# Score products of 64-dim heads over all 128 rows of the tensor engine, in two attention blocks of a four-layer kernel

## The chip, the core and the metric

The kernel runs on one core of a Trainium2 chip. The metric is the time of one execution in microseconds (us); less is better. The engines are named as the profile names them: PE (tensor engine, matmuls; PEld is its weight loads), DVE (vector engine), ACT (scalar engine), POOL (GpSimd), SP (the engine that issues DMAs). SBUF is the on-chip memory, PSUM the memory into which PE accumulates; both have 128 partitions.

## What is computed

The input is one sequence of 512 tokens with 1024 features. A first block (softmax attention, a gated delta rule, a gate) is left alone by the change. After it come two layers, each an attention and a feed-forward part (gate, up and down projection, 2816 wide), all in float32. The two attentions are what the change touches:

```python
# layer 0: stick breaking, 16 heads of 64; per block of 128 queries
z = einsum('bqhd,bkhd->bhqk', q_blk, k) * 64 ** -0.5
earlier = key_pos[None, :] < q_pos[:, None]
log_keep = where(earlier, log_sigmoid(-z), 0.0)
log_after = cumsum(log_keep, axis=3, reverse=True) - log_keep
weight = where(earlier, exp(log_sigmoid(z) + log_after), 0.0)
out = einsum('bhqk,bkhd->bqhd', weight, v)

# layer 1: differential attention, 8 heads with two maps of 64 dims each, values of 128
a = softmax(q1 k1 / 8) - lam * softmax(q2 k2 / 8)     # visible: key chunk of 64 <= query chunk
out = einsum('bhqk,bkhd->bqhd', a, v)                  # then an rms norm over the head
```

## The kernel before

**Matmuls in parts.** A product of float32 operands is made of three products in the type float32r: each operand is split into a rounded part `hi` and a rest `lo`, and `hi hi + hi lo + lo hi` accumulate in one PSUM bank (`mm3`, L307). `split` (L314) makes `hi` by a copy on ACT and `lo` by a subtraction on DVE. Weights come from DRAM as 512 KB tiles by DMAs on SP's queue and are split in the same way (`wtile`, L322). A few products, such as the one with the values, are plain float32, for which PE has two rows in the trace, each with a weight load.

**Order of the work.** Each part of a layer is a set of generators ("streams"). A `Driver` (L87) runs them in one thread at build time and so fixes the order of PE's instructions: it keeps a model clock, adds a cost for each matmul (L293), and always continues the stream that is ready first by that clock, the streams listed first before the others. A stream yields a number (us until its next operands are there), an event, or a place of a resource (PSUM banks: 2 for projections, 5 called `z`, 1 called `o`). So `SB_LAT1 = 5.0` and `DF_LAT1 = 4.0` are what the order allows for the elementwise work between two of a unit's PE steps. The projections are the last stream of each block: they fill PE's time between the attention steps. Nothing at run time changes this order; an engine works its instructions off in order, each waiting for its semaphores. Tiles of 128 x 512 float32 ("chunks") come from one pool of 57.

**Stick breaking** (`stick`, L601). Two heads (a pair `hp`, 8 pairs) share one chunk of 128 features: the head `s` = 0 has partitions 0 to 63, the head 1 has 64 to 127. A projection of q or k is evacuated in `evac_qk`: a multiply by the norm on DVE (L614), `hi` on ACT (L615), `lo` on DVE (L616), so each pair has four chunks (`sb_qhi`, `sb_qlo`, `sb_khi`, `sb_klo`). The event of the pair is set 2.6 us after its key projection (L660). The values are projected for four heads at once with tokens on partitions (`evac_v`, L620; for the first `first_v`, L626); ACT scales them (`scale_tm`, L571).

A `unit` (L664) handles one head and a bank of key tiles: b = 2 holds the key tiles 2 and 3 (256 and 128 query columns), b = 1 tile 1 (384), b = 0 tile 0 (512). For each key tile it makes the scores, three products of 64 rows and a mask (L680 to L683):

```python
self.mm(zz, k[0][d, ks], q[0][d, P * i:], j == 0, False)     # d: the head's 64 partitions
self.mm(zz, k[0][d, ks], q[1][d, P * i:], False, False)
self.mm(zz, k[1][d, ks], q[0][d, P * i:], False, False)
self.mm(zz[:, :P], self.neg30, self.m_ge, False, False)
```

Then come three functions on ACT (L686 to L688), a combination on DVE (L689) and a split into `sh` and `sl` on DVE; after `SB_LAT1` the sums over later keys are made on PE by triangular and all-minus-one matrices (L701, L703) in the same bank, ACT takes the exponential (L705), and PE multiplies by the values (L717) into the pair's `po` bank, each head into its own 64 partitions, with 64 columns of weights.

**Differential attention** (`diff`, L1814). q and k are projected with tokens on partitions, normed and rotated (`rotate`), transposed on PE in `to_fm` (L1892) and split there on ACT (L1902) and DVE (L1903); the event and the bank's release follow after 2.2 us (L1906, L1907). Head `j` has map 0 on partitions 0 to 63 and map 1 on 64 to 127. A `unit` (L1909) handles a head and one block of 128 queries (i = 3 down to 0, so 512 to 128 visible keys): for each map three products of 64 rows and a mask of 64 columns (L1925 to L1928), the row maximum on DVE (L1930), the exponential with its sum on ACT (L1935); then a combination of both maps on DVE (L1945), transposes on PE, a copy by ACT or DVE (L1953, L1955), and the product with the values (L1967).

Of the kernel before, what the change touches and what calls it, by code (L numbers as in the profile page):

```python
# [17 lines left out]
P = 128  # L18
# [40 lines left out]
# 500000 ** (-j / 8) as float32 has it  # L59
# [5 lines left out]
def two_pi_parts():  # L65
    """2 pi as parts of 8, 12 and 24 bits"""
# [18 lines left out]
class Slots:  # L85
    """free places of a resource, each with the time from which it is free"""
# [4 lines left out]
class Take:  # L91
    """n places of Slots at once"""
# [4 lines left out]
class Driver:  # L97
    """Merges the streams of work into one order of the tensor engine's instructions.

    A stream is a generator; it yields the microseconds until its next step's operands are there, an  # L100
    Event to wait for, or Slots of which it takes one."""
# [66 lines left out]
class Net:  # L168
    def __init__(self, ctx, tc, ins, out):
# [7 lines left out]
        # weights of the next proj_multi  # L177
# [3 lines left out]
        # the results of projections wait for this event  # L181
# [25 lines left out]
    def phase(self, name, **sizes):  # L207
        """pools of one part of the kernel"""
# [38 lines left out]
    def cmask(self, name, cmp, mult, base, val, dt=F32R):  # L247
        """val where base + mult*p + (-mult)*j  cmp 0, else 0"""
# [9 lines left out]
    def consts(self):  # L258
# [5 lines left out]
        # rows 0..63: 1, the others 0  # L264
# [7 lines left out]
        # [p, j]: 1 where p >= j, p <= j, p > j, p < j  # L272
# [4 lines left out]
        # columns 0..15 of the rows 16..31 of every 32  # L277
# [3 lines left out]
        # p - 32 b >= 16 and p - 32 b < 32, b by block of columns: one of the four is the row's own  # L281
# [40 lines left out]
    def wtile(self, ap, n=1024):  # L322
        """weights of one tile: [128, n] from DRAM, as two parts"""
# [11 lines left out]
    def wtile_big(self, ap):  # L335
        """weights [128, 1024] in chunks of 512 columns"""
# [1827 lines left out]
```

## Time and profile before

| what | value |
|---|---|
| median of 3 runs | 2264.87 us (2253.7 to 2268.81) |
| span of the profiled execution | 2268.6 us |
| PE busy | 2210.7 us, 97% of the span, 13342 matmuls |
| PE weight loads busy | 1855.4 us, 82% |
| DVE busy | 1212.9 us, 53% |
| ACT busy | 963.9 us, 42% |
| POOL busy | 95.5 us, 4% |
| DMA | 181.72 MB, mean 80 GB/s |

The span runs from the first to the last instruction of one execution, taken by the profiler; the page gives no other time for that execution. A share of busy time is an average over stages. Matmuls are pipelined and their ends are modelled, so the rows of PE overlap: what a matmul costs is the distance from its start to the next one's start. The granted clock is the share of TensorE's full clock that it got in a stretch; it has two levels, 1.2 and 2.4 GHz.

### The profile page before, as it was taken

To read this page: it belongs to the slowest core of one execution; us is meant where nothing else is said; L and a number is where in the kernel's file an instruction comes from. 1 tells how busy PE (TensorE), PEld (TensorE's weight loads), DVE (VectorE), ACT (ScalarE), POOL (GpSimd) and SP (SyncE) were. 2 spreads that over 40 slices of the span, in tenths; PEclk is the share of its full clock that TensorE was granted. 3 is DMA by queue.
4 is the path that set the end of the run, shared out by engine and by line. 5 is a ranking of instruction groups with operands and counts; after the bars stand their busy time and mean duration, and the time that the engine had idled before them with its cause. 6 is when DMAs were issued, how large, how long until landed. Compare 5 with 4: busy or idle time off the path is not lost.

```text
span 2268.6 us, 33416 instructions
## 1 busy us (share of the span) xinstructions
PE 2210.7 (97%) x13342; PEld 1855.4 (82%) x13342; DVE 1212.9 (53%) x2487; ACT 963.9 (42%) x1951; POOL 95.5 (4%) x109
## 2 busy tenths in 40 slices
PE   7999999989999998999999999999999999999999
PEld 6898898878888787777778888888999878888887
DVE  7865865976424567443346444433566656444421
ACT  5646666565423454544444223222444444232221
POOL 2000100000000000000000000000111100000000
PEclk9999999999999998899989999999898889999999
DMA  4221211323243521011103232233211113322332
GB/s 162 63 72 48 64 52 57 91 60 100 79 149 120 184 92 38 28 47 47 47 19 103 94 102 93 90 101 98 66 57 40 36 38 103 102 93 94 97 112 70
DMA packets 73995, 181.72 MB, mean 80 GB/s; under 512 B 24176, under 2 KB 24816, under 8 KB 73840
## 3 DMA queue, kind: packets, MB, share of 16 engines
q1 hardware_dynamic: 72560, 175.40, 24.2%
q0 software_dynamic: 1280, 4.20, 0.6%
q8 instruction: 105, 1.72, 0.3%
q14 instruction: 50, 0.41, 0.1%
HBM read 170.13 MB, written 9.44 MB: 79 GB/s over the span
## 4 chain that ended last, share of the span: by engine, by line
PE 84%; DVE 8%; ACT 3%; issue 1%; POOL 1%; DMA 1%; SPq 0%; DVEq 0%; ACTq 0%; POOLq 0%
PE pg L301 16%; PE pd L301 11%; PE pu L301 11%; PE po L301 9%; PE z L301 5%; PE pv L301 4%; PE pb L301 4%; PE s L301 3%; PE pz L301 2%; PE pq L301 2%; PE sb_q L301 2%; PE pk L301 2%; PE sb_k L301 2%; PE wS L301 2%; DVE cacc L818 1%
## 5 line engine op out<-in xcount | busy, mean ns | idle before, releaser
L317 ACT CAST whi<-st 128x1024 fp32r<-128x1024 f32 (+1 forms) x295 | 306.0, 1039 | 791.4 <-issue 340.3
L320 DVE TENSOR_TENSOR wlo<-st,whi 128x1024 fp32r<-128x1024 f32 (+1 forms) x295 | 355.9, 1208 | 284.8 <-ACT whi L317 280.9
L301 PE MATMUL pg<-rlo,whi 128*128 128x512 f32 x352 | 138.8, 394 | 0.0
L301 PE MATMUL pg<-rhi,whi 128*128 128x512 f32 x352 | 138.1, 392 | 0.0
L301 PE MATMUL pg<-rhi,wlo 128*128 128x512 f32 x352 | 138.0, 392 | 0.0
L301 PE MATMUL pd<-mh,whi 128*128 128x512 f32 x352 | 137.6, 391 | 0.0
L301 PE MATMUL pd<-mh,wlo 128*128 128x512 f32 x352 | 137.6, 391 | 0.0
L301 PE MATMUL pd<-ml,whi 128*128 128x512 f32 x352 | 137.5, 391 | 0.0
L301 PE MATMUL pu<-rhi,wlo 128*128 128x512 f32 x352 | 137.2, 390 | 0.0
L301 PE MATMUL pu<-rlo,whi 128*128 128x512 f32 x352 | 137.1, 390 | 0.0
L301 PE MATMUL pu<-rhi,whi 128*128 128x512 f32 x352 | 137.0, 389 | 0.0
L2032 DVE TENSOR_TENSOR sg<-pg,rfm 128x512 f32<-128x512 f32 x44 | 30.4, 691 | 118.5 <-PE pg L301 118.4
L2038 DVE TENSOR_TENSOR m<-pu,sg 128x512 f32<-128x512 f32 x44 | 30.4, 691 | 115.2 <-PE pu L301 115.2
L689 DVE SCALAR_TENSOR_TENSOR t<-z,t 128x384 f32<-128x384 f32 (+1 forms) x48 | 28.2, 600 | 99.8 <-ACT t L688 97.6
L301 PEld LDWEIGHTS pg<-rhi,wlo 128*128 128x128 f32 x352 | 66.2, 188 | 15.1 <-issue 0.5
L301 PEld LDWEIGHTS pg<-rlo,whi 128*128 128x128 f32 x352 | 66.3, 188 | 15.0 <-issue 0.5
L301 PEld LDWEIGHTS pg<-rhi,whi 128*128 128x128 f32 x352 | 66.2, 188 | 14.5
L301 PEld LDWEIGHTS pd<-ml,whi 128*128 128x128 f32 x352 | 66.2, 188 | 14.3
L301 PEld LDWEIGHTS pd<-mh,wlo 128*128 128x128 f32 x352 | 66.1, 188 | 14.3
L301 PEld LDWEIGHTS pd<-mh,whi 128*128 128x128 f32 x352 | 66.1, 188 | 14.2
L301 PEld LDWEIGHTS pu<-rhi,whi 128*128 128x128 f32 x352 | 66.1, 188 | 14.0
L301 PEld LDWEIGHTS pu<-rlo,whi 128*128 128x128 f32 x352 | 66.1, 188 | 14.0
(554 smaller groups left out, 5943.5 us busy)
## 6 DMA issues: line engine op xcount, KB each, us to landing
st<-w_gate SPq DMA_DIRECT2D x44, 512.0 KB, 3.4
st<-w_up SPq DMA_DIRECT2D x44, 512.0 KB, 3.4
st<-w_down SPq DMA_DIRECT2D x32, 512.0 KB, 3.5
st<-w_dn SPq DMA_DIRECT2D x24, 512.0 KB, 3.6
st<-w_out SPq DMA_DIRECT2D x24, 512.0 KB, 3.5
st<-w_down SPq DMA_DIRECT2D x16, 384.0 KB, 3.1
x<-xT SPq DMA_DIRECT2D x16, 256.0 KB, 5.9
st<-w_aq SPq DMA_DIRECT2D x8, 512.0 KB, 3.5
```

What stands on the lines that cost most here:

```text
L301: self.nc.tensor.matmul(out, lhsT=lhsT, rhs=rhs, start=start, stop=stop, skip_group_check=True)
L317: nc.scalar.copy(hi, src)
L320: nc.vector.tensor_tensor(lo, src, hi.bitcast(F32), op=ALU.subtract)
L689: nc.vector.scalar_tensor_tensor(out=t, in0=zz, scalar=0.0, in1=t, op0=ALU.max, op1=ALU.add)
L818: nc.vector.scalar_tensor_tensor(out=acc[:, a], in0=raw[:, b], scalar=w[:, s:s + 1], in1=acc[:, a], op0=ALU.mult, op1=ALU.add)
L2032: nc.vector.tensor_tensor(sg, ps, self.rfm, op=ALU.mult)
L2038: nc.vector.tensor_tensor(m, ps, sg, op=ALU.mult)
```

## The change

The scores of both blocks are made of two products over 128 rows instead of three over 64. A new function `stack` lays out the operands of one pair of heads (or of the two maps of a differential head). For each head the query's chunk holds its `hi` on the head's own 64 partitions and its `lo` on the other 64; the first key chunk `kh` holds the key's `hi` on both halves; the second, `kl`, holds the key's `lo` on the own half and zeros on the other. So `kh` with the query's chunk gives `hi hi + hi lo`, and `kl` gives `lo hi`. A pair now has six chunks instead of four.

Stick breaking's values are stored with 128 columns per head: for an even head the 64 values and 64 zeros, for an odd head 64 zeros and the 64 values, so that the product with the values writes all 128 partitions of `po` for either head; the two heads accumulate in one group. A group of four heads has four chunks of values instead of two. The zeros are written by POOL. `first_v` keeps its raw copy in a work tile instead of a chunk.

In `to_fm` the event and the release of the bank now follow after 3.0 us instead of 2.2; the 2.6 us of `stick` stay. Comments and docstrings are gone throughout. Line numbers in this text up to the prediction are those of the file before.

```diff
+    def stack(self, box, j, query, src, sc):
+        nc = self.nc
+        for s in range(2):
+            own, other = slice(64 * s, 64 * s + 64), slice(64 - 64 * s, 128 - 64 * s)
+            f = sc if isinstance(sc, float) else sc[own]
+            x = src[own]
+            hi = self.chunk("qs" if query else "kh", F32R)
+            nc.scalar.mul(hi[own], x, f)
+            if query:
+                lo = hi[other]
+                box[j, "q", s] = hi
+            else:
+                t = self.chunk("kl", F32R)
+                nc.gpsimd.memset(t[other].bitcast(F32), 0.0)
+                lo = t[own]
+                box[j, "kh", s], box[j, "kl", s] = hi, t
+            nc.vector.scalar_tensor_tensor(out=lo, in0=x, scalar=f, in1=hi[own].bitcast(F32),
+                                           op0=ALU.mult, op1=ALU.subtract)
+            if not query:
+                nc.scalar.mul(hi[other], x, f)
...
             def evac_qk(hp, wn, sc, ps):
-                hi = self.chunk(wn + "hi", F32R)
-                lo = self.chunk(wn + "lo", F32R)
                 t = self.work("qk")
                 nc.vector.tensor_tensor(t, ps, self.rfm, op=ALU.mult)
-                nc.scalar.mul(hi, t, sc)
-                nc.vector.scalar_tensor_tensor(out=lo, in0=t, scalar=sc, in1=hi.bitcast(F32),
-                                               op0=ALU.mult, op1=ALU.subtract)
-                qk[hp, wn] = (hi, lo)
+                self.stack(qk, hp, wn == "sb_q", t, sc)
+
+            def pad_v(g, b, ps):
+                for i in range(2):
+                    t = v[g, 2 * b + i] = self.chunk(f"v{2 * b + i}")
+                    nc.gpsimd.memset(t.rearrange("p (a k) -> p a k", a=2)[:, :, 64:192], 0.0)
+                    nc.scalar.mul(t.rearrange("p (a k d) -> p a k d", a=2, k=4)[:, :, 0::3],
+                                  ps[:, i * 256:(i + 1) * 256].rearrange("p (a k d) -> p a k d", a=2, k=2),
+                                  self.rt[:, 2 * b + i:2 * b + i + 1])
...
-                t = v[0, b] = self.chunk(f"v{b}")
+                t = self.work(f"v{b}raw")
                 nc.vector.tensor_copy(t, ps)
 
                 def rest():
-                    self.scale_tm(t, t, self.rt, b)
+                    pad_v(0, b, t)
...
-            hcol = 64 * ((2 * hp + s) % 4)
+            hcol = 128 * ((2 * hp + s) % 4)
...
-                self.mm(zz, k[0][d, ks], q[0][d, P * i:], j == 0, False)
-                self.mm(zz, k[0][d, ks], q[1][d, P * i:], False, False)
-                self.mm(zz, k[1][d, ks], q[0][d, P * i:], False, False)
+                self.mm(zz, kh[:, ks], q[:, P * i:], j == 0, False)
+                self.mm(zz, kl[:, ks], q[:, P * i:], False, False)
                 self.mm(zz[:, :P], self.neg30, self.m_ge, False, False)
...
-                vt = v[g, i // 2][:, (i % 2) * 256 + hcol:(i % 2) * 256 + hcol + 64]
-                self.mm(po[d, P * i:], vt, w[:, c0:c0 + T - P * i], i == 3, i == 0)
+                self.mm(po[:, P * i:], v[g, i][:, hcol:hcol + P], w[:, c0:c0 + T - P * i], s == 0 and i == 3, s == 1 and i == 0)
...
         def to_fm(w, j):
...
-            hi = self.chunk(w + "hi", F32R)
-            lo = self.chunk(w + "lo", F32R)
-            nc.scalar.mul(hi, ps, gv)
-            nc.vector.scalar_tensor_tensor(out=lo, in0=ps, scalar=gv, in1=hi.bitcast(F32),
-                                           op0=ALU.mult, op1=ALU.subtract)
-            fm[w, j] = (hi, lo)
-            drv.set(ev_fm[w, j], 2.2)
-            drv.release(self.free["z"], 2.2)
+            self.stack(fm, j, w == "q", ps, self.fv[:, self.col["g" + w]:self.col["g" + w] + 1])
+            drv.set(ev_fm[w, j], 3.0)
+            drv.release(self.free["z"], 3.0)
...
-                self.mm(zz, q[0][d, qs], k[0][d, :n], True, False)
-                self.mm(zz, q[1][d, qs], k[0][d, :n], False, False)
-                self.mm(zz, q[0][d, qs], k[1][d, :n], False, False)
+                self.mm(zz, q, fm[j, "kh", m][:, :n], True, False)
+                self.mm(zz, q, fm[j, "kl", m][:, :n], False, False)
                 self.mm(z[:, n - 64:n], self.neg30, self.m_half, False, True)
```

## Rows read from the trace of the kernel before

**Rows 1.** The page: the chain that ended last, shares of the span by engine.

```profile
PE 84%; DVE 8%; ACT 3%; issue 1%; POOL 1%; DMA 1%; SPq 0%; DVEq 0%; ACTq 0%; POOLq 0%
```

**Rows 2.** Windows: length, busy (rows) of PE, PEld, DVE, ACT, POOL; clock, DMA, GB/s.

```profile
900.00:1190.00 290.00, 289.77 (x1370) 218.40 (x1368) 124.10 (x210) 135.06 (x253) 0.00 (x0) 0.91 0.11 37
1203.00:1580.00 377.00, 377.00 (x1650) 309.74 (x1649) 165.80 (x197) 112.06 (x141) 0.00 (x0) 1.00 0.31 95
1590.00:1880.00 290.00, 288.03 (x1818) 252.79 (x1817) 175.68 (x590) 125.25 (x259) 35.33 (x25) 0.87 0.16 51
```

**Rows 3.** Timeline of PE, score products of stick breaking: start, us, instruction.

```profile
976.92 0.38 PE L301 MATMUL z<-sb_qhi,sb_khi 64*128 64x256 f32 x1
...
977.73 0.33 PE L301 MATMUL z<-sb_qhi,sb_khi 64*128 64x128 f32 x1
...
978.46 0.44 PE L301 MATMUL z<-sb_qhi,sb_khi 64*128 64x384 f32 x1
...
979.43 0.49 PE L301 MATMUL z<-sb_qhi,sb_khi 64*128 64x512 f32 x1
979.77 0.39 PE L301 MATMUL z<-sb_qlo,sb_khi 64*128 64x512 f32 x1
980.00 0.39 PE L301 MATMUL z<-sb_qhi,sb_klo 64*128 64x512 f32 x1
980.32 0.33 PE L301 MATMUL z<-m_ge,neg 128*128 128x128 f32 x1
980.58 0.38 PE L301 MATMUL z<-sb_qhi,sb_khi 64*128 64x256 f32 x1
```

**Rows 4.** Timeline of PE, the sums over later keys and the value product.

```profile
988.91 0.28 PE L301 MATMUL z<-sl,negones 128*128 128x128 f32 x1
989.02 0.33 PE L301 MATMUL z<-sh,negones 128*128 128x256 f32 x1
989.19 0.28 PE L301 MATMUL z<-sl,negones 128*128 128x256 f32 x1
989.31 0.34 PE L301 MATMUL z<-sh,negones 128*128 128x384 f32 x1
...
989.66 0.39 PE L301 MATMUL z<-sh,m_ntri 128*128 128x512 f32 x1
989.89 0.40 PE L301 MATMUL z<-sl,m_ntri 128*128 128x512 f32 x1
990.21 2.37 PE L301 MATMUL po<-w,v 128*64 128x128 f32 x8
992.51 0.33 PE L301 MATMUL z<-sh,negones 128*128 128x128 f32 x1
```

**Rows 5.** Timeline of PE, score products of the differential block, at both clock levels.

```profile
1689.33 0.50 PE L301 MATMUL s<-khi,qhi 64*128 64x512 f32 x1
...
1690.44 0.50 PE L301 MATMUL s<-khi,qhi 64*128 64x512 f32 x1
...
1698.41 0.47 PE L301 MATMUL s<-khi,qhi 64*128 64x128 f32 x1
...
1699.48 0.56 PE L301 MATMUL pk<-whi,rlo 128*128 128x256 f32 x1
```

**Rows 6.** Windows: a run of score products, what follows, and two bursts.

```profile
979.20:982.60 3.40, 3.40 (x17) 2.49 (x16) 2.02 (x5) 3.40 (x8) 0.00 (x0) 1.00 0.00 0
982.60:986.00 3.40, 3.40 (x10) 2.48 (x9) 3.23 (x7) 2.25 (x6) 0.00 (x0) 0.51 0.00 0
976.90:995.40 18.50, 18.50 (x86) 13.35 (x85) 9.61 (x18) 10.80 (x22) 0.00 (x0) 0.91 0.16 55
1689.30:1721.50 32.20, 32.20 (x138) 24.89 (x137) 18.57 (x65) 11.90 (x34) 0.26 (x1) 0.68 0.10 33
```

**Rows 7.** Groups of instructions by form: busy us, mean ns, idle before.

```profile
L1082 ACT COPY Pt<-Q 64x512 f32<-64x512 f32 x8 | 4.6, 578 | 1.3 <-PE Q L301 1.2
...
L616 DVE SCALAR_TENSOR_TENSOR sb_klo<-qk,sb_khi 128x512 fp32r<-128x512 f32 x8 | 5.5, 685 | 0.1
```

More of the change, by code (lines that the diff above doesn't have):

```diff
@@ L610, in evac_qk @@
             def evac_qk(hp, wn, sc, ps):
-                hi = self.chunk(wn + "hi", F32R)
-                lo = self.chunk(wn + "lo", F32R)
                 t = self.work("qk")
                 nc.vector.tensor_tensor(t, ps, self.rfm, op=ALU.mult)
-                nc.scalar.mul(hi, t, sc)
-                nc.vector.scalar_tensor_tensor(out=lo, in0=t, scalar=sc, in1=hi.bitcast(F32),
-                                               op0=ALU.mult, op1=ALU.subtract)
-                qk[hp, wn] = (hi, lo)
+                self.stack(qk, hp, wn == "sb_q", t, sc)
[6 more added lines that the diff above has]
+                                  self.rt[:, 2 * b + i:2 * b + i + 1])
             def evac_v(g, b, ps):
-                t = v[g, b] = self.chunk(f"v{b}")
-                self.scale_tm(t, ps, self.rt, b)
+                pad_v(g, b, ps)
                 if b == 1:
@@ L664, in unit @@
         def unit(hp, s, b, me, prev, head, pair):
-            d = slice(64 * s, 64 * s + 64)
             its = ((2, 0), (3, 256)) if b == 2 else ((b, 0),)
@@ L674, in unit @@
             yield self.free["z"]
-            q, k = qk[hp, "sb_q"], qk[hp, "sb_k"]
+            q, kh, kl = qk[hp, "q", s], qk[hp, "kh", s], qk[hp, "kl", s]
             z = self.bank("z", f"z{b}")
@@ L1898, in to_fm @@
                 self.transpose(ps[:, t * P:(t + 1) * P], tm[w, j // 2, t // 2][:, s:s + P])
-            gv = self.fv[:, self.col["g" + w]:self.col["g" + w] + 1]
-            hi = self.chunk(w + "hi", F32R)
-            lo = self.chunk(w + "lo", F32R)
-            nc.scalar.mul(hi, ps, gv)
-            nc.vector.scalar_tensor_tensor(out=lo, in0=ps, scalar=gv, in1=hi.bitcast(F32),
-                                           op0=ALU.mult, op1=ALU.subtract)
-            fm[w, j] = (hi, lo)
-            drv.set(ev_fm[w, j], 2.2)
-            drv.release(self.free["z"], 2.2)
+            self.stack(fm, j, w == "q", ps, self.fv[:, self.col["g" + w]:self.col["g" + w] + 1])
+            drv.set(ev_fm[w, j], 3.0)
+            drv.release(self.free["z"], 3.0)
         def unit(j, i, me, prev, head):
@@ L1915, in unit @@
                 yield prev["S"]
-            q, k = fm["q", j], fm["k", j]
             es = []
@@ L1920, in unit @@
                 yield self.free["z"]
-                d = slice(64 * m, 64 * m + 64)
-                qs = slice(P * i, P * i + P)
+                q = fm[j, "q", m][:, P * i:P * i + P]
                 z = self.bank("z", f"s{m}")
                 zz = z[:, :n]
-                self.mm(zz, q[0][d, qs], k[0][d, :n], True, False)
-                self.mm(zz, q[1][d, qs], k[0][d, :n], False, False)
-                self.mm(zz, q[0][d, qs], k[1][d, :n], False, False)
+                self.mm(zz, q, fm[j, "kh", m][:, :n], True, False)
+                self.mm(zz, q, fm[j, "kl", m][:, :n], False, False)
                 self.mm(z[:, n - 64:n], self.neg30, self.m_half, False, True)
```

## The prediction

> **What bounds the kernel now.** I read the page's chain first: 84% of the span is the tensor engine (PE), 8% the vector engine (DVE), 3% the scalar engine (ACT) [rows 1]. Only two blocks are touched, so I then read the windows by stage. Stick breaking runs from about 900 to 1190 us, the differential block from about 1590 to 1880. In both PE has work in flight for practically the whole time (289.8 and 288.0 of 290 us), while ACT is busy 135 and 125 us and DVE 124 and 176 [rows 2]. So PE sets the pace. The reader should see one more thing there: in the feed-forward stage between them PE is just as busy and its granted clock is 1.00, while in the two blocks it is 0.91 and 0.87 [rows 2].
>
> Busy time of PE hides what a matmul costs, since ends are modelled and rows overlap. So I took the timeline and read from start to start, in one burst of score products [rows 3]. One head of stick breaking (key tiles of 256, 128, 384 and 512 columns, each three half-row products and a mask) takes 0.81 + 0.73 + 0.97 + 1.15 = 3.66 us at the full clock. The products themselves stream at 0.23 us for 512 columns. But the first one of a group takes 0.34 until the next starts, the third 0.32 to the mask, and the mask, 128 columns, 0.26 until the next group (980.58 less 980.32). Full-row products standing among their own kind cost 0.11, 0.12, 0.17 and 0.23 us for 128, 256, 384 and 512 columns, with no such gap [rows 4]. So each change between half-row and full-row products costs some 0.1 to 0.15 us, and there are two per group.
>
> The clock: PE is busy 3.40 of 3.40 us in the run of half-row products from 979.2 at clock 1.00, then again 3.40 of 3.40 at 0.51 in the stretch behind it [rows 6]. In the burst of the differential block from 1689.3 it is 0.68 on the mean [rows 6]. The engine fell to the lower of its two levels (1.2 of 2.4 GHz) without an idle moment, behind products that use half its rows. Where all rows are used it stays up [rows 2].
>
> **The change part by part.** *Stick breaking's scores.* Three half-row products become two full-row ones per key tile, and nothing changes mode. A head then costs 2 x (0.11 + 0.12 + 0.17 + 0.23) + 4 masks x 0.11 = 1.70 us instead of 3.66. Times 16 heads: 31 us less.
>
> *Differential scores.* The first group of 512 columns takes 1.11 us [rows 5] where stick's takes 1.15, so I put a head-half at 3.66 - 4 x 0.04 = 3.5 us; afterwards 1.70 as above. Times 16: 29 us less.
>
> *Stick's value product.* The weights grow from 64 to 128 columns by zeros, the moving columns stay. A head's eight rows (two per fp32 product) take 2.30 us from 990.21 to 992.51, and the row before them 0.32 instead of 0.23 [rows 4]. The streaming stays; only the change into and out of 64-column products goes, about 0.2 us. Times 16: 3 us. If the wider weights were not hidden behind the moving columns it could cost a few us instead, so I bound it by -5 and +5.
>
> *The clock.* A mean of 0.91 and 0.87 over 290 us each is 26 + 38 = 64 us of full-speed work lost [rows 2]. That is the upper bound. Half-row groups don't lose as much as that: a 128-column group takes 1.07 us at the lower level (1698.41 to 1699.48) against 0.73 at the upper [rows 3, 5], 1.47 times rather than twice. If everything lost only so much, it would be 64 x 0.64 = 41 us. I take 54, between the two, as those stretches hold both kinds. Full-row products fill these stretches as projections do at 1.00, so I expect nearly all of it back; the lower bound is 0.
>
> Sum so far: 31 + 29 + 3 + 54 = 117 us.
>
> *Added work.* For each pair of heads `stack` issues six ACT multiplies instead of two and four DVE subtractions instead of two, each on 64 partitions, and two POOL memsets. Half the partitions don't halve the time: a 64x512 copy on ACT takes 0.58 us and the 128x512 subtraction on DVE 0.69 [rows 7], and I take the latter for 64 partitions too. For 16 pairs that is 64 x 0.58 = 37 us of ACT and 32 x 0.69 = 22 of DVE. Stick's ACT goes from 135 to some 153 of a block of about 240 us, diff's DVE from 176 to 187 of about 245: below PE, so their throughput is covered by PE. What stands on the path is the latency of the last pieces: the scores wait in PE's order behind `sb_k`'s stacked key. The work order gives that 2.6 us (L660); a multiply by the norm, four ACT pieces and one DVE piece are 0.69 + 4 x 0.58 + 0.69 = 3.7. About 1 us per pair could be late, 8 us in stick if the projections placed between don't cover it. In `to_fm` the allowance rises from 2.2 to 3.0, and I cost it at 0 there; behind the stacking on ACT stand the exponentials, on DVE the maxima, whose waiters are PE's transposes. The memsets run on POOL, busy 0.00 and 35 of 290 us [rows 2]; no row shows one of this size, so I put them at ACT's 0.58 us at the most: 32 of them and 16 of the value tiles would be 28 us if nothing covered them, and I take 0. No DMA is added and SP's queue is unchanged.
>
> *What is late next.* PE's order is fixed when the kernel is compiled, so once PE is faster it can come too early. In stick's burst (976.9 to 995.4) ACT is busy 10.8 of 18.5 us and DVE 9.6 [rows 6], so there is room; I take 0 to 2 us per head pair for this and the stacked key together, 1 on the mean: 8 us. In the differential burst of two heads DVE is busy 18.6 of 32.2 us [rows 6]. PE's work there, 32.2 x 0.68 = 21.9 us at full speed, loses four times 1.8, which leaves 14.7: less than DVE's 18.6. So DVE's chain (maximum, reciprocal, combination, copy) ends last there, at 18.6 or later. The shortfall is 4 us and more unless projections stand between; four such bursts (two heads each) give 0 to 24 us, and I take 3 each, 12 in all. Such waits may drop the clock again now and then: 0 to 12, I take 5.
>
> So 117 - 8 - 12 - 5 = 92 us. The profiled execution spans 2268.6 us, of which 92 is 4.05%; the three runs have a median of 2264.87 (2253.7 to 2268.81), and less 4.05% that is **2173 us**.
>
> One rule of the Trainium skill speaks against the change ("TensorEngine Tiling (Array Packing)", Overview and Key Properties): with 64 rows or fewer the array splits into two tiles that work in parallel, up to 2x. By it three half-row products would cost as little as one and a half full ones, two full ones would then be dearer, and by that rule the sum falls by some 30 us, to 2203. The rows don't show it: 512 half-row columns take 0.23 us to the next start, as 512 full-row ones do [rows 3, 4], since successive products use the same half. I keep the sum.
>
> **The rivals.** *All of it comes back:* no wait shows, because projections fill PE's gaps. For it: PE has matmuls in flight for 289.8 and 288.0 of 290 us now [rows 2], so the order leaves next to no wait. Against: DVE's 18.6 us. 117 us, or 127 with the whole clock loss: 2148 to 2138.
>
> *The clock stays where it is:* what lowers it is not the half rows but something the change leaves alone, such as the mix of short products. For it: projections stand between the groups at the lower level too [rows 5, 6]. Against: the fall lies right behind the half-row run. Then 63 - 20 = 43 us: 2222. The Trainium skill ("TensorE: Matmul & The Clock Gate", Part 1) has the clock follow how busy PE is, and PE is not idle in these rows; by that rule taken alone nothing would change for the clock, and this rival is what comes out.
>
> *Slower:* the stacking ends on the path. Place: between the last matmul of a key projection (or the transposes of `to_fm`) and the first score. Price: 4 x 0.58 + 2 x 0.69 = 3.7 us for each of 16 pairs, 59 us. It decides if, besides, the gaps around the groups are not of the mode but of the operands and stay, and the clock too; then only the third product goes, 32 x 0.63 = 20 us, and 2265 + 39 = 2304. Against: PE's order has projections in those places.
>
> *It doesn't act:* the gaps stay, and the waits eat the rest: about 2260.
>
> **How the numbers follow.** The forecast's own case (2150 to 2205) gets 0.62, all of it back 0.15, the clock stays 0.17, slower 0.03, no action 0.03. The first three are faster by over 1% (some 23 us, about what a measurement of this kernel can tell from no change): 0.94; within it 0.03; slower 0.03. The range goes from 2138, the sum with the whole clock loss and no wait, to 2222, the clock's rival.
>
> **What would show it.** Right: score rows read 128*128 and stand 0.23 us apart for 512 columns, a mask 0.11 from the next group; stick's block is some 235 us long and the differential one some 245; granted clock 0.97 or more in both; ACT busier by some 20 us in each. DVE would be what ends PE's few waits in the differential bursts. Wrong: a clock near 0.9 still (the clock's rival), PE waiting for the stacked key behind each key projection for over 2 us, or bursts of the differential block still 30 us long.

## The result, and the profile after

The kernel after the change takes 2179.6 us (median of 4 runs, 2178.7 to 2184.1), the kernel before beside it 2266.8 (4 runs). The ratio is 0.961, with a 95% interval of 0.958 to 0.965. The forecast was 2173, within 2138 to 2222. The profiled execution spans 2177.9 us, 90.7 less than the 2268.6 of before; 92 had been forecast between the two.

First the page of the kernel after: busy time by engine, and further down the chain that ended last.

```profile
PE 2101.2 (96%) x13214; PEld 1804.9 (83%) x13214; DVE 1231.3 (57%) x2519; ACT 1000.5 (46%) x2015; POOL 117.0 (5%) x157
...
PE 79%; DVE 11%; ACT 5%; issue 2%; POOL 2%; DMA 1%; SPq 0%; POOLq 0%; DVEq 0%; ACTq 0%
```

PE's share of the chain falls from 84 to 79% [rows 1], DVE's rises from 8 to 11. ACT is busy 36.6 us longer than before and DVE 18.4; the forecast had 37 and 22.

Then the windows, with the columns of [rows 2]: stick breaking, the feed-forward part behind it, the differential block.

```profile
897.00:1130.00 233.00, 231.64 (x1330) 198.23 (x1330) 134.64 (x226) 153.43 (x287) 13.01 (x29) 1.00 0.14 46
1140.00:1510.00 370.00, 370.00 (x1620) 303.90 (x1619) 166.40 (x198) 112.11 (x141) 0.00 (x0) 1.00 0.31 97
1532.00:1790.00 258.00, 239.71 (x1789) 226.27 (x1788) 187.96 (x611) 147.26 (x294) 43.76 (x41) 0.97 0.19 60
```

Two things changed. The granted clock is 1.00 and 0.97 where it was 0.91 and 0.87. And PE, which had next to no idle time in either block, now idles 18.3 us of 258 in the differential one, but only 1.4 of 233 in stick.

To see where the time went I cut the span at the first product of each block's first projection; the last part runs to the end:

| | first block | stick | feed-forward | differential | feed-forward |
|---|---|---|---|---|---|
| before, us | 871.8 | 351.3 | 362.7 | 316.1 | 366.6 |
| after, us | 876.1 | 293.3 | 362.7 | 279.1 | 366.6 |
| difference | +4.3 | -58.0 | 0 | -37.0 | 0 |

So the two blocks give 95.0 us. The first block, in which the order of PE's work is the same, takes 4.3 back. In the profiles of this study it was 868.7 to 878.8 us long with the stacked operands and 869.9 to 878.3 without them, so I don't count these 4.3 us to the change.

The timeline of PE in the kernel after, one score group of 512, of 256 and the start of one of 128 columns (start, length, instruction):

```profile
928.20 0.45 PE L301 MATMUL z<-qs,kh 128*128 128x512 f32 x1
928.49 0.40 PE L301 MATMUL z<-qs,kl 128*128 128x512 f32 x1
928.73 0.22 PE L301 MATMUL z<-m_ge,neg 128*128 128x128 f32 x1
928.78 0.33 PE L301 MATMUL z<-qs,kh 128*128 128x256 f32 x1
928.95 0.28 PE L301 MATMUL z<-qs,kl 128*128 128x256 f32 x1
929.07 0.22 PE L301 MATMUL z<-m_ge,neg 128*128 128x128 f32 x1
929.13 0.28 PE L301 MATMUL z<-qs,kh 128*128 128x128 f32 x1
```

From start to start the group of 512 takes 0.58 us (1.15 before [rows 3]), that of 256 takes 0.35 (0.81). The forecast's spacing gives 2 x 0.23 + 0.11 = 0.57 and 2 x 0.12 + 0.11 = 0.35. The gaps at the mask are gone: it stands 0.24 us behind the second product of 512 columns and 0.05 us ahead of the next group, whose first product then takes a little longer (0.17 for 256 columns); the sum is as forecast.

### The profile page after: what moved, and what is told of

The parts are those of the page before. It is cut to its first block, busy times and chain, and to the rows that moved or that the text cites. A ratio compares the mean times of both kernels' runs of the same rounds, so it can differ in the third digit from the quotient of the medians.

```text
span 2177.9 us, 33391 instructions
## 1 busy us (share of the span) xinstructions
PE 2101.2 (96%) x13214; PEld 1804.9 (83%) x13214; DVE 1231.3 (57%) x2519; ACT 1000.5 (46%) x2015; POOL 117.0 (5%) x157
## 4 chain that ended last, share of the span: by engine, by line
PE 79%; DVE 11%; ACT 5%; issue 2%; POOL 2%; DMA 1%; SPq 0%; POOLq 0%; DVEq 0%; ACTq 0%
PE pg L301 17%; PE pd L301 11%; PE pu L301 11%; PE po L301 8%; PE pb L301 4%; PE z L301 3%; PE pv L301 3%; PE pz L301 3%; PE wS L301 2%; PE pk L301 2%; DVE wlo L320 2%; DVE cacc L845 2%; PE sb_q L301 2%; PE sb_k L301 1%; PE s L301 1%
## 5 line engine op out<-in xcount | busy, mean ns | idle before, releaser
L301 PE MATMUL pv<-whi,rhi 128*128 128x256 f32 x256 | 75.9, 297 | 3.3 <-ACT tmq L1868 2.1
```

The source lines that it names most:

```text
L301: self.nc.tensor.matmul(out, lhsT=lhsT, rhs=rhs, start=start, stop=stop, skip_group_check=True)
```

## The experiments

Each kernel was timed beside the kernel before on the same chip; its ratio is to that. Where a mask is changed to 64 rows, the cuts below leave out a line `drv.t += 0.052` behind it: it gives the `Driver`'s model clock the time of the old mask, so that the order of PE's work stays.

### Do the two parts add up?

The first kernel has the change in stick breaking alone; `diff` is that of the kernel before.

> The change in stick breaking alone; the differential block is that of the kernel before. The two traces put 58.0 us of the gain into stick (351.3 to 293.3 us) and 37.0 into the differential block (316.1 to 279.1). Theory: the blocks don't touch each other, so 2267 - 58 = 2209 us, within 5; granted clock 1.00 in stick and below 0.9 in the differential block. Rival: the blocks share buffers, and one lengthens the other (the first block was 4.3 us longer after the change): 2214 us or more, with the first block at 876 us again rather than 872.

It took 2218.4 us (4 runs), ratio 0.978 (0.976 to 0.980). Stick is 293.4 us long, as after the change; the differential block 317.3, as before it, and the first block 877.7. 2268.6 - 57.9 + 1.2 + 5.9 gives the 2217.7 us of its span but for 0.1 of rounding. Both signs of the rival came, a time above 2214 and a first block near 876, and the time misses the theory's 2204 to 2214. Yet the two blocks have the lengths that the theory gives them, and the excess is the first block alone. Later profiles speak against the rival's reason: a kernel below that stacks nothing (whole masks on half rows) has a first block of 878.3 us, and one that stacks (`DF_LAT5` at 7) has 868.7.

### Row changes, half rows, number of products: a square

Three things differ between a score group of before and of after: rows per product (64 or 128), row changes inside the group (two or none) and number of products (three or two). Four kernels take them apart.

Changes alone, with two full-row products (the same edit in `stick` and `diff`):

```diff
-                self.mm(zz[:, :P], self.neg30, self.m_ge, False, False)
+                self.mm(zz[:, :P], self.neg30[:64], self.m_ge[:64], False, False)
...
-                self.mm(z[:, n - 64:n], self.neg30, self.m_half, False, True)
+                self.mm(z[:, n - 64:n], self.neg30[:64], self.m_half[:64], False, True)
```

> The changed kernel with the mask product over 64 rows instead of 128; stick breaking's mask so leaves out its lower 64 rows of keys, the differential one is the same sum. The scores stay full-row products, and each of the 128 groups gains two changes between full-row and half-row products. Theory (a change costs 0.1 to 0.15 us by itself): 128 x 2 x 0.1 to 0.15 = 26 to 38 us more, 2206 to 2218, less what falls into PE's waits in the differential block; the granted clock stays at 0.95 or more, since half-row products are few. Rival 1 (the gaps around a group of before were of the operands or of the accumulation, not of the row count): no change, 2180. Rival 2 (it is the change of rows that lowers the clock): clock 0.9 or less in both blocks and 2230 or more.

2216.3 us, ratio 0.978 (0.976 to 0.981): 37 us more than the kernel after, 33.5 of it in the two blocks (stick +21.5, differential +12.0). For stick's 64 groups the 21.5 are 0.34 us a group, 0.17 a change, a little over the forecast's 0.1 to 0.15. Rival 1 is out: a change of rows costs time by itself. Rival 2 is out in its size, with the clock at 0.99 and 0.98, but not wholly. Two windows of this kernel in stick; all 15 rows of the first are of score groups:

```profile
1040.70:1044.10 3.40, 3.40 (x15) 2.19 (x14) 0.94 (x3) 2.84 (x7) 0.00 (x0) 1.00 0.22 88
1044.10:1050.90 6.80, 6.80 (x17) 5.05 (x17) 3.70 (x8) 4.77 (x10) 0.00 (x0) 0.50 0.02 4
```

Here the clock fell once, for 6.8 us, right behind full-row products with half-row masks between them, without an idle moment of PE. There is one more such fall in the differential block, 3.4 us long at 1737.0. In stick of the kernel before there are eight (the stretch at the lower level around the block's start, which every profile here has, isn't counted).

Half rows without changes, in the kernel before (`d` are the head's own 64 partitions):

```diff
-                self.mm(zz[:, :P], self.neg30, self.m_ge, False, False)
+                self.mm(zz[:, :P], self.neg30[d], self.m_ge[d], False, False)
...
-                self.mm(z[:, n - 64:n], self.neg30, self.m_half, False, True)
+                self.mm(z[:, n - 64:n], self.neg30[d], self.m_half[d], False, True)
```

> The kernel before with the mask products on the 64 rows of the head's scores, so that a group has no change of row count inside; the mask so leaves out a part of its keys or, for the second map of the differential block, is empty. Still three half-row products a group. Theory (row changes cost time, half rows lower the clock): groups stand closer, 128 groups with one to two changes less, 0.1 to 0.15 us each, 13 to 38 us less at the full clock; the clock falls as before or further (0.85 to 0.9), which takes some of it back: 2235 to 2260. Rival 1 (the changes cost nothing): 2267. Rival 2 (the changes lower the clock, not the half rows): clock 0.97 or more in both blocks and 2190 to 2200.

2198.2 us, ratio 0.970 (0.968 to 0.973), far below my 2235 to 2260, and in time just at rival 2 (its clock of 0.97 came in stick, not in the differential block). Three half-row products a group, the order of before, no stacking, and 75.2 of the 95.0 us of the two blocks are there. Windows of this kernel, the two blocks:

```profile
905.00:1170.00 265.00, 262.99 (x1450) 206.70 (x1449) 132.91 (x221) 140.38 (x263) 0.00 (x0) 1.00 0.16 50
1545.00:1818.00 273.00, 264.38 (x1878) 241.02 (x1877) 182.34 (x602) 131.22 (x268) 35.36 (x25) 0.94 0.18 58
```

The clock is 1.00 in stick with half-row products. That contradicts the forecast's reason for the clock. Its timeline shows something else that was not visible before, where the groups of two heads (first on partitions 0 to 63, second on 64 to 127) meet; "x2" stands for two rows of one kind, here the one of the first head and the one of the second, with the shape of the earlier:

```profile
1030.34 0.44 PE L301 MATMUL z<-sb_qhi,sb_khi 64*128 64x512 f32 x2
1030.57 0.44 PE L301 MATMUL z<-sb_qlo,sb_khi 64*128 64x256 f32 x2
1030.68 0.28 PE L301 MATMUL z<-sb_qhi,sb_klo 64*128 64x256 f32 x1
1030.80 0.22 PE L301 MATMUL z<-m_ge,neg 64*128 64x128 f32 x1
1030.85 0.39 PE L301 MATMUL z<-sb_qhi,sb_klo 64*128 64x512 f32 x1
1030.86 0.27 PE L301 MATMUL z<-sb_qhi,sb_khi 64*128 64x128 f32 x1
1030.97 0.27 PE L301 MATMUL z<-sb_qlo,sb_khi 64*128 64x128 f32 x1
1031.08 0.22 PE L301 MATMUL z<-m_ge,neg 64*128 64x128 f32 x1
1031.08 0.27 PE L301 MATMUL z<-sb_qhi,sb_klo 64*128 64x128 f32 x1
1031.19 0.27 PE L301 MATMUL z<-m_ge,neg 64*128 64x128 f32 x1
1031.31 0.39 PE L301 MATMUL z<-sb_qhi,sb_khi 64*128 64x384 f32 x1
```

Between 1030.34 and 1031.31 a whole group of 512 columns runs beside groups of 256 and of 128. One after the other, at the spacings of [rows 4] with 0.06 for a mask that stands without a gap (929.07 to 929.13 in the kernel after), they would need 0.75 + 0.42 + 0.39 = 1.56 us by this estimate; they take 0.97. Two half-row products on different halves ran at the same time. The Trainium skill says that they can ("TensorEngine Tiling (Array Packing)", Key Properties: different tiles can execute in parallel), and the rows agree. It also says there that a change of tiling mode drains the engine; the 0.17 us a change above fits that. In the kernel before, a full-row mask stood behind every group, and so between the heads too: there its changes showed, and the parallel run could not.

Three products on full rows, without changes:

```diff
                 self.mm(zz, kl[:, ks], q[:, P * i:], False, False)
+                self.mm(zz, kl[:, ks], q[:, P * i:], False, False)
...
                 self.mm(zz, q, fm[j, "kl", m][:, :n], False, False)
+                self.mm(zz, q, fm[j, "kl", m][:, :n], False, False)
```

> The changed kernel with a third full-row product in each group (the one of kl is made twice, so the scores count that part twice). Same number of products per group as before the change, but all of them on 128 rows. Theory: 32 head-halves x (0.11 + 0.12 + 0.17 + 0.23 = 0.63 us) = 20 us more, less what falls into PE's waits in the differential block: 2190 to 2200, granted clock 0.97 or more in both. So the third product would be some 20 us of the gain and rows and clock the rest. Rival (the number of short products lowers the clock): clock about 0.9 in both blocks, 2230 or more.

2193.9 us, ratio 0.967 (0.965 to 0.969), stick 302.3 us and the differential block 284.0, clock 1.00 and 0.99. The third product is 9.0 us in stick (the forecast's 0.63 x 16 = 10) and 4.9 in the differential block, where the rest falls into PE's waits. The rival falls.

The fourth kernel: three products on full rows, with changes. It is the edits of the first and of the third of these kernels together. (Its expectation says that changes alone had not lowered the clock; the two falls above are what that leaves out.)

> Three full-row products (that of kl twice) and the mask over 64 rows (in stick breaking its lower 64 rows of keys are left out): the same number of products, columns and row changes per group as in the kernel before, with rows full and half exchanged. It closes a square: half rows with changes (before: stick 351.3 us, differential 316.1), half rows without (307.6, 284.6), full rows without (302.3, 284.0). Half rows alone have not lowered the clock in stick, nor have changes alone in the kernel with two products and a half-row mask. Theory A (what lowers the clock is that the stream of columns pauses at the changes for as long as it takes to make a whole run of such groups slow, whatever the rows): the clock falls as in the kernel before, stick 340 us or more, 2245 to 2270. Theory B (half rows and pauses are both needed): the clock holds at 0.97 or more, and only the changes cost, 64 x 0.33 = 21 us in stick and 12 to 21 in the differential block above the kernel with three full-row products: 2225 to 2237.

2223.2 us, ratio 0.979 (0.975 to 0.982): theory B, a little under its 2225. One group of 512 columns, from 977.19 to 978.34, and the windows of the two blocks:

```profile
977.19 0.50 PE L301 MATMUL z<-qs,kh 128*128 128x512 f32 x1
977.52 0.63 PE L301 MATMUL z<-qs,kl 128*128 128x512 f32 x2
978.09 0.33 PE L301 MATMUL z<-m_ge,neg 64*128 64x128 f32 x1
978.34 0.39 PE L301 MATMUL z<-qs,kh 128*128 128x256 f32 x1
```

```profile
905.00:1190.00 285.00, 284.40 (x1480) 230.18 (x1479) 151.93 (x246) 167.83 (x302) 10.61 (x26) 1.00 0.14 47
1565.00:1848.00 283.00, 272.17 (x1874) 244.64 (x1874) 197.65 (x618) 154.86 (x300) 44.75 (x41) 0.98 0.17 55
```

The group takes 1.15 us, to the hundredth what the half-row group of before takes [rows 3]. Number of products, columns, changes and duration are the same; only full and half are exchanged. Yet the clock is 1.00 here and 0.91 there. So the same pauses at the changes that went with eight falls between half rows went with none here; nor (kernel with half rows and no changes) did half rows alone bring one in stick. That it takes both together would say too much, since the kernel with two products and changes fell once in stick. One thing besides the rows differs between this kernel's stick and that of before, the value product with its 128 columns instead of 64. The falls of before stand right behind score groups [rows 6], and in the differential block, whose value product is the same in both kernels, the clock is 0.98 here and 0.87 before.

The square, as lengths of the two blocks in us and granted clock of their windows:

| products per group | with row changes | without |
|---|---|---|
| three, half rows | 351.3 and 316.1, clock 0.91 and 0.87 (before) | 307.6 and 284.6, 1.00 and 0.94 |
| three, full rows | 321.0 and 295.2, 1.00 and 0.98 | 302.3 and 284.0, 1.00 and 0.99 |
| two, full rows | 314.8 and 291.1, 0.99 and 0.98 | 293.3 and 279.1, 1.00 and 0.97 (after) |

The stick of the two kernels with half rows also holds the value product with 64 columns, some 8 us by the rows in the part on why.

### Was the half-row kernel fast for what it left out?

The kernel with half rows and no changes left out part of its masks. A version with whole masks, made on the head's own 64 rows by a matrix `neg_sw` (the identity times -1e30 with its column halves exchanged):

```diff
-                self.mm(zz[:, :P], self.neg30, self.m_ge, False, False)
+                self.mm(zz[:, :P], self.neg30[d], self.m_ge[d], False, False)
+                if s == 0:
+                    self.mm(zz[:, :64], self.neg_sw[d], self.m_half[d], False, False)
+                    self.mm(zz[:, 64:P], self.neg_sw[d], self.m_ge[d, :64], False, False)
+                else:
+                    self.mm(zz[:, :64], self.neg_sw[d], self.m_ge[d, 64:], False, False)
...
-                self.mm(z[:, n - 64:n], self.neg30, self.m_half, False, True)
+                self.mm(z[:, n - 64:n], (self.neg_sw if m else self.neg30)[d], self.m_half[d], False, True)
```

> The kernel before with its whole masks made on the 64 rows of the head's own scores: in stick breaking by two or three short products instead of one of 128 rows, in the differential block by one with the identity's halves exchanged for the second map. Nothing is left out; no group changes the row count inside; the scores stay three half-row products and nothing is stacked. Theory (changes of rows, and the lower clock behind runs of such groups, are what the change removed): as in the kernel with partial masks (2198), plus 96 more short products of 0.03 to 0.06 us: 2195 to 2208, granted clock 0.97 or more. Rival (that kernel was fast for what it left out of the masks): 2230 or more, clock 0.95 or less.

2216.4 us, ratio 0.977 (0.974 to 0.979): between the theory and its rival. The differential block, where the mask only changed its place, is 281.5 us long, so nothing had hung on what was left out there. Stick is 331.5 instead of 307.6, and its clock has fallen again, though no group changes rows. Windows of this kernel: stick, then the first half of a run of score groups and what follows, its second half among it.

```profile
905.00:1200.00 295.00, 294.10 (x1574) 236.86 (x1573) 139.16 (x228) 148.08 (x272) 0.38 (x1) 0.95 0.14 45
...
978.90:982.10 3.20, 3.20 (x28) 3.10 (x28) 0.00 (x0) 1.59 (x4) 0.00 (x0) 1.00 0.41 147
982.10:985.50 3.40, 3.40 (x18) 3.33 (x16) 3.02 (x7) 3.34 (x8) 0.00 (x0) 0.50 0.00 0
```

PE has work in flight throughout, at 1.00 and then at 0.50, as in [rows 6]; in the window of stick the clock falls six times in this way (the expectation below has seven). What this kernel adds to stick are products of 64 columns. The next kernel asks whether those lower the clock on full rows too:

```diff
                 self.mm(zz[:, :P], self.neg30, self.m_ge, False, False)
+                for c in ((0, 64) if s == 0 else (0,)):
+                    self.mm(zz[:, c:c + 64], self.neg30, self.m_ge[:, c:c + 64], False, False)
```

> The changed kernel with the short products that the kernel with exact half-row masks had in stick breaking, but on 128 rows: behind each mask one (second head) or two (first head) products of 64 columns that repeat a part of the mask, 96 in all. Nothing is left out. In that kernel the clock fell seven times in stick (0.95), in the kernel with partial half-row masks, which lacks these short products, not at all. Theory (half-row products and a loose stream are both needed): full rows hold the clock at 1.00 in stick, and the 96 products cost 0.05 to 0.11 us each, 5 to 11 us: 2184 to 2192. Rival (short products lower the clock whatever the rows): clock 0.97 or less in stick, 2195 or more.

2189.0 us, ratio 0.963 (0.961 to 0.965). Stick is 303.1 us long, 9.8 more than the 293.3 of the kernel after, which is 0.10 us for each of the 96 products, and its clock is 1.00:

```profile
905.00:1170.00 265.00, 263.00 (x1503) 225.05 (x1502) 149.49 (x243) 164.57 (x302) 12.01 (x29) 1.00 0.15 50
```

So in stick no fall of the clock came where every product of the groups had full rows, with short products or without, and with full-row scores and row changes one came in one of two kernels. With half rows it fell eight times with changes and six with short products, and not at all where the products stood close and two heads ran in part side by side. Whether it was the closeness or the second half of the rows at work beside the first that held the clock there, no run separates. In the differential block half rows without changes have 0.94 and 0.96 against 0.99 with three full-row products. With half rows (partial masks) the three falls there last 6.8 to 13.7 us and follow waits of PE of 0.7 to 0.9 us; with three full-row products two falls of 3.4 us follow waits of 2.2 and 2.4. That points to the rows, but the waits differ as well, and it stays open.

### Is the stacking on the path?

```diff
             if not query:
-                nc.scalar.mul(hi[other], x, f)
+                nc.gpsimd.memset(hi[other].bitcast(F32), 0.0)
```

> The changed kernel with the other half of each stacked key written by POOL as zeros instead of by ACT as a second copy, so that key hi by query lo is left out of the scores. Theory (the stacking lies beside the projections and costs PE nothing): 2177 to 2182. Rival (its last ACT pieces are late for the scores, as the forecast's 8 us for stick had it): 2172 or less, with the stick block shorter by 5 us or more.

2174.0 us, ratio 0.957 (0.954 to 0.960), against 0.961 (0.958 to 0.965) for the kernel after; it lies between the theory and its rival. The stick block is 292.6 us long, 0.7 less than after the change: the last ACT piece of each key, the one that this edit takes away, is covered there, and the forecast's 8 us were not there to win. In the differential block it is 276.3, 2.8 less. PE's waits show why: its wait for ACT's copy of a projection, L1868, falls from 2.1 us (below) to 0.2. The ACT pieces stand ahead of that copy in ACT's order, and until it is done a bank of PE's projections is not free. They cost more than the 0.58 us of [rows 7]; the groups of the kernel after by line, reading PSUM and reading SBUF:

```profile
L624 ACT ACTIVATE kh<-tr,fv 64x512 fp32r<-64x512 f32 x16 | 10.9, 684 | 2.0 <-DVE kl L621 1.0
L624 ACT ACTIVATE kh<-qk 64x512 fp32r<-64x512 f32 x16 | 10.1, 631 | 0.4
```

### Where PE waits in the differential block

The waits of PE in the kernel after, 1532 to 1800 us (what PE was to do, what it waited for, us in total, times, longest):

```profile
PE otr L305 <- DVE os L2005: 10.7, 5, 2.5
PE tp L305 <- DVE e L1963: 2.8, 2, 1.9
PE pv L301 <- ACT tmq L1868: 2.1, 4, 1.0
PE tp L305 <- DVE sums L1958: 1.4, 3, 0.5
PE po L301 <- ACT ohi L2016: 0.8, 1, 0.8
```

17.8 us in all; the same view of before has 1.9. The largest is `otr`, the transposes of a head's normed output, which wait for the last step of that norm on DVE (L2005). Windows of the kernel after around one such wait, with the columns of [rows 2]:

```profile
1628.00:1662.40 34.40, 33.91 (x270) 32.51 (x269) 29.19 (x103) 21.49 (x53) 4.32 (x4) 1.00 0.20 62
1662.40:1664.80 2.40, 0.30 (x4) 0.10 (x2) 1.60 (x6) 0.00 (x0) 0.93 (x1) 1.00 0.00 0
1665.90:1669.40 3.50, 3.50 (x19) 3.50 (x18) 1.97 (x14) 1.06 (x2) 2.58 (x3) 0.51 0.00 0
```

DVE is busy 29.2 of the 34.4 us ahead of it, with the norm's small steps between the next group's rotations and weight splits. Then PE has 0.3 us of work in 2.4 while POOL (the power) and DVE finish the norm, and right after that the clock is at 0.51 for 3.5 us. The order allows `DF_LAT5` = 4 us from the last step to the transposes. Two kernels give it more:

```diff
-DF_LAT5 = 4.0
+DF_LAT5 = 7.0
```

> The changed kernel with DF_LAT5 at 7 us instead of 4: the order then places 3 us more of projections between the norm of a differential head's output and its transposes, for which PE waited 10.7 us in five places in the trace after the change. Theory (this chain is the shortfall in the differential block): those waits go and the clock falls behind them with them, 8 to 14 us less, 2166 to 2172. Rival (DVE's amount of work in the bursts is the limit, 27 to 31 us busy of 34 to 38): the waits move to another place, 2176 to 2182.

2175.2 us (6 runs, 2167.9 to 2178.9), ratio 0.958 (0.955 to 0.961). The differential block is 275.0 us long instead of 279.1; the rest of what its profile gains is a first block of 868.7. Its waits:

```profile
PE pv L301 <- ACT tmq L1868: 6.3, 4, 2.5
PE otr L305 <- DVE os L2005: 3.8, 2, 2.5
PE tp L305 <- DVE e L1963: 3.5, 2, 2.6
```

`otr` loses 6.9 us and `pv` and `tp` gain 4.9. The wait moves rather than goes.

```diff
-DF_LAT3 = 3.0
+DF_LAT3 = 5.0
...
-DF_LAT5 = 4.0
+DF_LAT5 = 6.0
```

> The changed kernel with DF_LAT3 at 5 us instead of 3 and DF_LAT5 at 6 instead of 4: DVE's multiplication by the head's factor is placed later in DVE's order too, and the transposes later in PE's. Theory (the wait for this chain is the shortfall): 8 to 14 us less, 2166 to 2172, and less of DVE's other work waits behind it than with the 7 alone. Rival (amount of DVE work): 2176 to 2182.

2178.5 us, ratio 0.959 (0.957 to 0.962), the block 278.4 us: nothing. `otr` waits 3.9 us here, but `pv` 3.8 and the transposes `tr` 2.7. The rival has it in this kernel, and most of it in the one above.

The wait for L1868 had gone when the stacking was taken from ACT. So the next kernel has `DF_LAT5` at 7 and lets POOL write the second half of each stacked key, as a copy:

```diff
-                nc.scalar.mul(hi[other], x, f)
+                nc.gpsimd.tensor_copy(hi[other], hi[own].bitcast(F32))
```

> DF_LAT5 at 7 as before, and the second half of each stacked key made by POOL as a copy of the first half instead of by ACT as a second product with the factor. Theory (with the norm's wait gone, PE's next wait is for ACT's copy at L1868, 6.3 us in four places, behind the stacking pieces; zeros by POOL took it to 0.2): the differential block falls from 275 to some 270 us, 2166 to 2172. Rival (POOL is slow at it, and its powers for the norms, 1.0 to 1.6 us each, come later): the differential block is as long or longer, 2176 or more.

The kernel after ran beside it once more:

> The changed kernel itself once more, beside the two others. Expected: 2175 to 2184, stick block 293, differential block 279. It shows how much of 4 us is run to run; the first block, which the change leaves alone, has been 869 to 879 us long in the profiles so far.

With the copy on POOL: 2171.5 us (6 runs, 2170.4 to 2178.2), ratio 0.957 (0.955 to 0.959). The kernel after: 2180.4 (4 runs, 2176.5 to 2182.7), ratio 0.960 (0.958 to 0.963). The two intervals overlap, but the profiles agree on the place: the differential block is 270.7 us long against 279.4, stick 294.2 against 293.8. Its waits in the differential block, and POOL's copies:

```profile
PE otr L305 <- DVE os L2005: 3.8, 2, 2.5
PE tp L305 <- DVE e L1963: 3.5, 2, 2.6
PE pv L301 <- ACT tmq L1868: 1.9, 2, 1.2
```

```profile
L624 POOL CAST kh<-kh 64x512 fp32r<-64x512 f32 x32 | 32.6, 1020 | 181.7 <-ACT kh L612 180.7
```

A copy takes POOL 1.02 us, more than ACT's 0.63 to 0.68, but nobody waits for POOL there. Its median is the lowest of the study.

## Why the prediction came out right, and where it was not

**Score products.** Right in size, and shown part by part. The forecast took 31 us from stick's scores, about 10 of it for the third product and 21 for the changes. Measured: 9.0, and 18.7 to 21.5 for the changes (three and two products a group).

**The value product.** Undersized, though no kernel tried it by itself. The rows around one run of eight, before (beginning with 989.89 and 990.21 in [rows 4]) and after:

```profile
992.68 0.27 PE L301 MATMUL z<-sl,negones 128*128 128x128 f32 x1
```

```profile
976.82 0.39 PE L301 MATMUL z<-sl,m_ntri 128*128 128x512 f32 x1
...
979.27 0.27 PE L301 MATMUL z<-sl,negones 128*128 128x128 f32 x1
```

Between the same two neighbours it is 992.68 - 989.89 = 2.79 us before and 2.45 after, 0.34 less; in the half-row kernel without changes, which keeps the 64 columns, 2.8 to 3.0. The value products stand in 24 such runs in the timeline of before, not 16, so an estimate from these rows is 24 x 0.34 = 8 us. The forecast had 3, and 5 as its bound.

**The clock: right in size, wrong in its reason.** The sum took 54 us and left 5 in later falls, 49 net. By the windows 26 + 38 us were lost before at the most, and 0 + 258 x 0.03 = 8 after: 56 back, by the same bound. The square prices it more closely. With changes, half rows instead of full ones make stick 30.3 us longer, of which 8 are the value product's, so 22, and the differential block 20.9: 43 us, with the longer waits of PE in that block already taken off. The step that failed is the sentence that the engine fell "behind products that use half its rows" and "Where all rows are used it stays up". The second half held in stick: the clock fell in no kernel in whose groups every product had full rows. The first did not: with half rows and close products the clock was 1.00 there. Half rows went with a fall where the stream was loose too, by changes of rows (before) or by short products; and full-row scores fell once where half-row masks stood between them. The forecast's rival, that something which the change leaves alone lowers the clock, is excluded by the clock after.

The Trainium skill has the clock follow how busy PE has been ("TensorE: Matmul & The Clock Gate", Part 1). The profile's busy time is not that measure: it is 100% in the run that fell in the kernel before, and in stick 284.4 of 285 us with full rows and changes, where the clock was 1.00. How rows and pauses share in a fall, these runs don't settle.

**Half rows in parallel.** The forecast set aside the rule of two parallel tiles, since the rows of before showed none and "successive products use the same half". The reason was right, and it had an end: where two heads met without a mask between them, the tiles did run in parallel. By this rule the forecast would have put the time after at 2203; it came out at 2179.6, because the rows of before paid for changes and didn't run side by side. The kernel that lets the rule act in part has 307.6 us in stick with part of its masks left out, some 8 of them the value product's. Two full-row products with whole masks are still cheaper, 293.3.

**Waits in stick.** Forecast 8 us, found some 1.4 (PE's idle time in the window). The work between projection and first score covers the stacking: the experiment with POOL's zeros won 0.7 us, and in PE's waits in stick after the change only 0.2 us are for a stacked operand (`qs`).

**Waits in the differential block.** The term was undersized: forecast 12 us, found 17.8 by the waits and 18.3 by PE's idle time, within its bounds of 0 to 24. The mechanism, DVE ending last once PE is faster, holds for 14.9 of the 17.8. The place was wrong: not "maximum, reciprocal, combination, copy" in the first line but the norm of the head's output, a chain over ACT, DVE and POOL that the forecast didn't list. And part of it hangs on ACT, as the POOL kernels show, through the pieces of `stack`, which the forecast had covered by PE's time on throughput alone. The score part of a burst did shrink, from 30.3 us (1689.33 [rows 5] to 1719.6) to 18.3:

```profile
1685.95 0.40 PE L301 MATMUL s<-kh,qs 128*128 128x512 f32 x1
...
1704.25 0.36 PE L301 MATMUL pk<-wlo,rhi 128*128 128x256 f32 x1
```

**The sum.** Split by block with the clock term in proportion to its bounds (22 and 32 us), the forecast had 48 us for stick (31 + 3 + 22 - 8) and 44 for the differential block, with the later falls put there (29 + 32 - 12 - 5). Stick gave 58.0 and the other 37.0. Stick's 10 too few are the 8 us taken off for waits, which hardly came, and 5 of the value product, less some 3 of the scores (9.0 + 18.7 = 27.7 us of 31). Of the 7 too many, 4 are waits (15.9 us more than before, where 12 had been taken); the rest isn't split. That 2173 is within 7 us of the result owes something to these two meeting.

## What to carry to other kernels

Look at the row count of neighbouring products on PE: a small full-row product between half-row ones (here a 128-column mask) cost 0.34 us a group by itself, more than the third score product (9.0 us for 64 groups, 0.14), and behind such groups with half rows the clock fell again and again as well. Filling the rows removed both. Keeping everything in a run on half rows is the cheaper edit where the operands can't be stacked, but with the whole masks it gave back much of its gain (2216 us), since short products came with them. When PE gets faster, list every chain that PE waits for, small norms on several engines included, and the copies that free its banks: lengthening one allowance alone moved the wait to the next chain.

## What the runs showed of the hardware that was not expected

- Half-row products of two heads, on opposite halves of the partitions, ran at the same time: an estimated 1.56 us of work in 0.97.
- A group of three products and a mask takes 1.15 us for 512 columns whether the products have half rows and the mask full ones or the other way round. The cost lies in the change, in either direction.
- Two stretches of stick whose score groups are equal in product count, columns, changes and duration had a clock of 0.91 (half rows) and 1.00 (full rows); with one product less, full rows and changes fell once. PE's busy time, practically full in all three, didn't tell which would fall.
- Going from products with 128 columns of weights to a run with 64 and back cost 0.34 us (2.79 against 2.45).
- A product of 64 columns on full rows adds 0.10 us, the same as 128 columns (0.11).
- POOL's zeros of 64x512 took 0.53 us each in the kernel after (16.9 us for 32), which no row of before had shown; nobody waited for them.
